# The recurrent mixer's 1/(1 - t): an exponential and a Newton step instead of RECIPROCAL

## The chip, the core and the metric

The kernel runs on one core of one Trainium2 chip. The metric is the device time of one execution in microseconds (us), as the median of several runs. The core has a matrix engine (TensorE, called PE in the profile, with its weight loads as PEld), a vector engine (VectorE, DVE), an engine for activation functions (ScalarE, ACT), a general engine (GpSimd, POOL) and a queue that issues transfers (SyncE, SP). Each engine works off its own instructions in the order in which they were queued; semaphores hold an instruction until what it needs is done, and everything behind it on that engine waits with it.

## What the reference computes

One layer on x of 1024 tokens by 1024 channels, in float32: an RMS norm, one projection `h @ w_in`, two mixers, a gated merge, an output projection and the residual. The first mixer is attention with compressed, selected and windowed keys (8 heads, 2 groups). The second is the recurrent mixer, on which the change works:

```python
uc = conv_b + sum(up[:, k:k + S] * conv_w[k] for k in range(CONV_WIDTH))
r = jax.nn.sigmoid(einsum(ub, lru_wa) + lru_ba)
i = jax.nn.sigmoid(einsum(ub, lru_wx) + lru_bx)
log_a = (-LRU_C * r) * jax.nn.softplus(-lru_lambda)
a = jnp.exp(log_a)
b = jnp.sqrt(-jnp.expm1(2.0 * log_a)) * (i * uc)
h_t = a_t * h_(t-1) + b_t
```

Its output is gated by silu and projected. 512 channels are four blocks of 128.

## The kernel before, in words

Every product is made of three matmuls on parts of float32 numbers, high and low (`mm3`, L169 to L172): high by high, high by low, low by high. `wload` (L174) fetches raw weights over the SP queue, `wsplit` (L179) splits them in two parts on ACT (L184) and on POOL or DVE (L185).

The program has these stages. First x is loaded, normed and transposed (to about 30 us of the span). Then come the recurrent mixer and the compressed keys, interleaved by hand in the order `ORD = "0c1c0c2c1c323"` (L45, L447): each digit takes the generator `lru(n)` of one block of 128 channels to its next `yield`, and `c` does so for `compress()`. The first half of `lru(n)` projects u and the gate, convolves, and splits uc in uh and ul (L336, L337). The second half makes the two gates r and i by matmuls into two PSUM banks named ps_t and a sigmoid each (L352), and then the element-wise chain that the change edits (L353 to L369), on tiles of 128 x 1024. With t = tanh(log_a / 2) (L356), a is (1 + t) / (1 - t) (L363) and sqrt(1 - a^2) is 2 sqrt(-t) / (1 - t) (L357, L364); 1 / (1 - t) is a subtraction (L361) and a RECIPROCAL (L362), both on DVE. Then i is multiplied by uc on POOL (L365) and by the square root on DVE (L366), the scan runs on DVE (L367), POOL multiplies by the gate (L368), and a transfer stores the block (L369). Tiles `t` (the helper `ta`) share nine buffers; the tile `kTs`, which holds the gate and i of a block, has one buffer, so block n + 1 waits for L368 of block n.

Then `qkv(0)` (L469) makes queries, keys and values of the first group, a token block at a time, from block 7 down to block 0, into five PSUM banks used in turn (four ps_s, one ps_f), two a token block. A bank is free when ACT (L498, L499) and DVE (the small copy of the branch gates, L500) have read it. `prep` (L522) takes each token block on: squares on ACT (L531), a sum on DVE (L533), an inverse root on POOL (L192, L193), scalings on DVE and POOL (L536 to L538), splits (L541 to L550), and transposes on PE (L554, L561) with copies on ACT and DVE (L556, L565). When the blocks 3 to 7 are prepared, the first attention scores follow (L612); the attention, with other products between as filling, lasts to about 700 us, and the merge and the output projection end the program. The bias tiles that the scores need are loaded over SP (L454, L458) into buffers of the name t.

What decides the order on every engine is not the program text alone: the context is opened with `schedule_with_timeline_sim=True` (L1103), a planner that orders the instructions by priority (place in the program) and by a timeline of its own. A changed instruction or dependence can so move others. Table loads on ACT (the functions that it can compute at a time) are put in where the order needs them.

Of the kernel before, what the change touches and what calls it, by code (L numbers as in the profile page):

```python
# [9 lines left out]
FT = mybir.dt.float32  # L10
FR = mybir.dt.float32r
AF = mybir.ActivationFunctionType
OP = mybir.AluOpType
# [29 lines left out]
LE = 1  # L43
IE = 0
# [5 lines left out]
CE = 0  # L50
# where the p of the units after the fourth lie in one tile
OFF = {(2, 1): 2560, (1, 1): 1536, (1, 0): 2560, (0, 1): 3584}
# [34 lines left out]
def _build(ctx, tc, A, out, dbg):  # L87
    nc = tc.nc
    dbg = dbg or {}
    V, C, G, T = nc.vector, nc.scalar, nc.gpsimd, nc.tensor  # L90
# [16 lines left out]

# [1 line left out]
    @contextmanager  # L109
# [17 lines left out]
    def ps_f(most):  # L127
        """the banks of the products beside the attention; more of them after it"""
        if tail:
            return next(tail[0])()[:, 0:most]  # L130
        return (ps("ps_f", PF) if PF else ps_s())[:, 0:min(most, FW)]
# [4 lines left out]
    def rotation():  # L136
        """the banks of scores and of those products, in turn"""
        n = PB[0] + PF
        return itertools.cycle([(lambda: ps("ps_f", PF)) if k * PF // n != (k + 1) * PF // n else ps_s for k in range(n)])
# [5 lines left out]

    # after the attention: banks and blocks that it held
    tail = []
# [31 lines left out]
    def wsplit(raw, k, into=None, E=None):  # L179
        """hi and lo parts of 1024 weights per partition, as [128, k, n]"""  # L180
        if into is None:
            into = [ST.tile([128, WTOK], FR, name=n, bufs=2)[:, :raw.shape[-1]] for n in ("w_hi", "w_lo")]
        hi, lo = into
        C.activation(hi, raw, AF.Copy)  # L184
        (E or (V if tail else G)).tensor_tensor(out=lo, in0=raw, in1=f(hi), op=OP.subtract)  # L185
        return [x.rearrange("p (k n) -> p k n", k=k) for x in (hi, lo)]
# [7 lines left out]

# [1 line left out]
    ident_r = K.tile([128, 128], FR, name="ident_r")  # L196
# [43 lines left out]

# [1 line left out]
    kcT = K.tile([128, 2, 2, 64], FR, name="kcT")  # L242
    vcc = K.tile([128, 2, 2, 64], FR, name="vcc")
    # the norms of heads are taken of sums, not means: (sum + 64 eps) ** -0.5. The queries' scale takes
    # the missing factor 8, the keys' gain gets it
    V.tensor_scalar(out=part["kgain"], in0=part["kgain"], scalar1=HD ** 0.5, scalar2=None, op0=OP.mult)
# [6 lines left out]
    def chunk_half(o, wh, wl, half):  # L253
        """o [128, 512] = w^T h^T, tokens of one half"""
        t = slice(half * 512, (half + 1) * 512)
        for kc in range(8):
            mm3(o, wh[:, kc], wl[:, kc], hT_h[:, kc, t], hT_l[half][:, kc], kc == 0, kc == 7)
# [9 lines left out]

# [1 line left out]
    rows_t = DR.tile([NH, NROW], FT, name="rows")  # L269
# [3 lines left out]
    for c0 in range(0, NROW, 512):  # L273
# [8 lines left out]
        dma(rows_t[:, c0:c0 + w], neg)  # L282
# [1 line left out]
    lp = part["lru_p"].rearrange("p (a n) -> p a n", n=4)  # L284
# [13 lines left out]

    # -4 softplus(-lambda): log1p by the series of atanh
    y = K.tile([128, 8, 4], FT, name="spt")  # L300
# [14 lines left out]
    m4sp = K.tile([128, 4], FT, name="m4sp")  # L315
    V.tensor_scalar(out=m4sp, in0=y[:, 5], scalar1=-8.0, scalar2=None, op0=OP.mult)

# [1 line left out]
    yb = DR.tile([4, 128, S], FT, name="yb")  # L319

    def lru(n):
# [31 lines left out]
        sc = m4sp[:, n:n + 1]  # L353
        # t = tanh(log_a / 2): a = (1 + t) / (1 - t), sqrt(1 - a^2) = 2 sqrt(-t) / (1 - t)
        a, q = ta(), ta()
        C.activation(a, r, AF.Tanh, scale=sc)  # L356
        C.activation(q, a, AF.Sqrt, scale=-1.0)  # L357
        if LE == 2:
            C.activation(r, a, AF.Copy, scale=-1.0, bias=1.0)
        else:  # L360
            EN[LE].tensor_scalar(out=r, in0=a, scalar1=-1.0, scalar2=1.0, op0=OP.mult, op1=OP.add)  # L361
        V.reciprocal(r, r)  # L362
        V.scalar_tensor_tensor(out=a, in0=a, scalar=1.0, in1=r, op0=OP.add, op1=OP.mult)  # L363
        V.scalar_tensor_tensor(out=q, in0=q, scalar=2.0, in1=r, op0=OP.mult, op1=OP.mult)  # L364
        EN[IE].tensor_tensor(out=i, in0=i, in1=uc, op=OP.mult)  # L365
        EN[JE >> n & 1].tensor_tensor(out=i, in0=i, in1=q, op=OP.mult)  # L366
# [4 lines left out]

# [1 line left out]
    def compress():  # L373
# [7 lines left out]
        for j in range(2):  # L381
# [3 lines left out]
            for g in range(2):  # L385
# [3 lines left out]
                for b in range(2):  # L389
                    # token 16 (c + b) + 2 l  # L390
                    dv = d.rearrange("p (c l s) -> p c l s", l=8, s=2)
                    V.tensor_tensor(out=flat[b][:, :, g, 0:63].rearrange("p l c -> p c l"),
                                    in0=dv[:, b:b + 63, :, 0],
                                    in1=pe[:, j, None, b * 8:(b + 1) * 8].to_broadcast([128, 63, 8]), op=OP.add)
# [54 lines left out]

# [1 line left out]
    bias = K.tile([128, NH, 256], FT, name="bias")  # L451
# [17 lines left out]
    def qkv(g):  # L469
        """q and the keys and values of both branches, tokens on partitions"""  # L470
        big = fr(p_slc())
# [12 lines left out]
        for tb in range(NT - 1, -1, -1):  # L484
# [21 lines left out]
            yield 0.655  # L506
        # sigmoid(z) = (1 + tanh(z / 2)) / 2: tanh is in every table that the neighbours use
        C.activation(bg[:, g], bg[:, g], AF.Tanh, scale=0.5)
# [13 lines left out]
    def prep(g, tb, e=None):  # L522
        """norms, the split in two parts and the transposes of one token block"""
        if e is None:
# [53 lines left out]
    def scores(g, i, br, st):  # L578
        """p [128, 4 heads, n keys] and the jobs that fill it, one per head; those of the first
        branch fill the compressed branch's p too"""  # L580
        b0 = max(0, i - 4) if br else 0
# [21 lines left out]
        def job(h):  # L603
# [4 lines left out]
            for c0, c1 in zip(cuts, cuts[1:]):  # L608
                s = ps_s()[:, 0:c1 - c0]
                for hl in range(2):  # L610
                    rhs = kT[1][hl][:, b0 * 128 + c0:b0 * 128 + c1] if br else kTs[:, hl, c0:c1]
                    T.matmul(s, qT[h][:, i * 128:(i + 1) * 128], rhs, start=(hl == 0), stop=(hl == 1))  # L612
                # the columns of s by where their bias comes from
                cc = 0
# [46 lines left out]
    def tr(p, c0):  # L661
        """p^T of 128 keys of the four heads, in two parts"""
        pt = ps_t()
# [9 lines left out]
    def tr_c(pc):  # L673
        """p^T of the compressed keys of the four heads: high parts over low parts"""
        pt = ps_t()
# [30 lines left out]
    def units(g):  # L706
        """(jobs, steps) of each unit; a step is a transpose and the product that follows it"""
        for i in range(NT - 1, -1, -1):
# [34 lines left out]
    def gated(half, y1):  # L743
        """y_a^T, gated, in two parts, tokens of one half"""
        tk = slice(half * 512, (half + 1) * 512)
# [14 lines left out]
    def merge(half, pa, m1, ya):  # L760
        """(y_a, projected, + the other mixer's part)^T, tokens of one half"""
        tk = slice(half * 512, (half + 1) * 512)
# [29 lines left out]
    def side_work():  # L792
        """products that wait for nothing: gates, then the recurrent mixer's projection"""
        seq = [("b", m) for m in range(8)] + [("n", m) for m in range(4)] + [("a", m) for m in range(8)]
# [5 lines left out]
        def more():  # L800
            """the next weights in two parts, and the load of those two after them"""
            c = len(ws)
# [6 lines left out]
        more()  # L809
        # by pairs at the end, the first half of the tokens first: what follows needs its place  # L810
        order = [(c, h) for c in range(18) for h in range(2)] + [(c, h) for h in range(2) for c in (18, 19)]
        for c, half in order:
# [4 lines left out]
            while q < 512:  # L817
# [4 lines left out]
                for kc in range(8):  # L822
                    mm3(o, wh[:, kc], wl[:, kc], hT_h[:, kc, t], hT_l[half][:, kc, tl], kc == 0, kc == 7)
                    if kc < 7:
                        yield w * 0.00126
                # tanh(z / 2) of a gate, z of g_nsa
                with urgent(UPE):
# [29 lines left out]
        for t4 in range(4):  # L857
# [23 lines left out]
            more()  # L881
        # the merge of the second half, whose attention ends first
        d2 = [t_l(0, 4), t_l(1, 4)]
# [34 lines left out]
    def attention():  # L918
# [12 lines left out]
        n = len(seq) // 2  # L931
        # the scores that go with the steps of each: those of the next
        ahead = {k: [k + 1] for k in range(2 * n)}
# [98 lines left out]

# [1 line left out]
def _bucket_table():  # L1034
    """which bucket each column of the bias rows takes, and where it is masked"""
    d = np.concatenate([np.arange(NF) - 127,
# [70 lines left out]
```

## Time and profile before

| what | value |
|---|---|
| timed runs | 908.88, 909.04 and 909.33 us, median 909.04 |
| profiled execution | span 908.0 us from the first to the last instruction; no time of its own beside the span is recorded, the median is 1.04 us above it |
| PE busy | 874.2 us, 96% of the span |
| DVE, ACT, POOL busy | 573.3, 439.1, 300.6 us |
| granted TensorE clock, mean | 0.994 of full speed |

Busy PE is not PE at its peak, since matmuls overlap. What is read from the profile is where PE stands idle, which wait ended last there, and what the engine that ended it was doing.

### The profile page before, as it was taken

How to read it: one execution, taken by the hardware profiler on the slowest of the kernel's cores; microseconds unless marked ns; L12 is line 12 of the kernel's file. 1: busy time of each engine (PE TensorE's matmuls, PEld its weight loads, DVE VectorE, ACT ScalarE, POOL GpSimd, SP SyncE). 2: the span in 40 equal slices, each digit the busy share in tenths (PEclk: the TensorE clock that was granted, in tenths of full speed). 3: DMA queues.
4: the chain of work that ended last, by engine and by line, in shares of the span. 5: the costliest groups of instructions: out<-in, count | busy, mean ns of one | idle time of the engine just before them, and what ended most of it. 6: DMA issues, size and time to landing. Idle time of an engine off the chain costs nothing.

```text
span 908.0 us, 15833 instructions
## 1 busy us (share of the span) xinstructions
PE 874.2 (96%) x5670; PEld 781.0 (86%) x5670; DVE 573.3 (63%) x1626; ACT 439.1 (48%) x1159; POOL 300.6 (33%) x339
## 2 busy tenths in 40 slices
PE   4999999989899999999999999999999899999998
PEld 3678878889899999999999998999999877888887
DVE  5642778897722447475687867677777886784111
ACT  6421434645523548575566666566667663321000
POOL 4122233169622325252455553243233421000000
PEclk9999999999999999999999999999999999999999
DMA  9215321121312112122121232111113469983111
GB/s 340 64 49 139 131 95 55 55 82 48 117 48 82 59 48 74 52 86 69 55 66 65 77 102 75 47 54 60 46 42 119 132 202 331 336 270 119 70 70 47
DMA packets 45519, 92.49 MB, mean 102 GB/s; under 512 B 6896, under 2 KB 12704, under 8 KB 45440
## 3 DMA queue, kind: packets, MB, share of 16 engines
q1 hardware_dynamic: 44480, 88.33, 28.9%
q0 software_dynamic: 960, 3.15, 0.9%
q8 instruction: 44, 0.72, 0.3%
q14 instruction: 35, 0.29, 0.1%
HBM read 64.15 MB, written 25.21 MB: 98 GB/s over the span
## 4 chain that ended last, share of the span: by engine, by line
PE 80%; DVE 7%; DMA 4%; POOL 4%; issue 2%; ACT 2%; SPq 0%; DVEq 0%; ACTq 0%; POOLq 0%
PE ps_f L170 9%; PE ps_f L171 9%; PE ps_f L172 9%; PE ps_s L612 7%; PE ps_s L170 7%; PE ps_s L171 7%; PE ps_s L172 7%; PE ps_t L665 6%; PE ps_t L170 4%; PE ps_t L171 4%; PE ps_t L172 4%; PE ps_o L690 3%; PE ps_o L689 3%; POOL ss L193 1%; DVE sq L536 1%
## 5 line engine op out<-in xcount | busy, mean ns | idle before, releaser
L171 PE MATMUL ps_f<-big_l,w_hi 128*128 128x256 f32 (+1 forms) x700 | 200.3, 286 | 0.0
L170 PE MATMUL ps_f<-big_h,w_hi 128*128 128x256 f32 (+1 forms) x664 | 193.8, 292 | 1.0 <-ACT ev L829 0.8
L172 PE MATMUL ps_f<-big_h,w_lo 128*128 128x256 f32 (+1 forms) x664 | 189.4, 285 | 0.0
L171 PEld LDWEIGHTS ps_f<-big_l,w_hi 128*128 128x128 f32 x700 | 131.9, 188 | 2.1
L170 PEld LDWEIGHTS ps_f<-big_h,w_hi 128*128 128x128 f32 x664 | 125.6, 189 | 4.1 <-ACT ev L829 2.3
L172 PEld LDWEIGHTS ps_f<-big_h,w_lo 128*128 128x128 f32 x664 | 125.4, 189 | 1.6
L670 DVE TENSOR_TENSOR pl<-ps_t,ph 128x512 fp32r<-128x512 f32 x132 | 90.4, 686 | 47.5 <-ACT ph L669 46.0
L185 POOL TENSOR_TENSOR w_lo<-w_raw,w_hi 128x1024 fp32r<-128x1024 f32 x33 | 80.7, 2448 | 102.1 <-ACT w_hi L184 101.7
L669 ACT ACTIVATE ph<-ps_t 128x512 fp32r<-128x512 f32 x132 | 78.1, 599 | 48.8 <-PE ps_t L665 45.6
L650 POOL TENSOR_SCALAR p_slc<-p_slc,mx,bg 128x384 f32<-128x384 f32 (+7 forms) x88 | 68.7, 786 | 89.5 <-DVE mx L649 34.8
L646 ACT ACTIVATE p_slc<-ps_s,mx 128x256 f32<-128x256 f32 (+5 forms) x128 | 68.1, 541 | 24.1 <-DVE mx L644 18.6
L171 PE MATMUL ps_s<-big_l,w_hi 128*128 128x512 f32 (+1 forms) x184 | 73.8, 401 | 0.0
L184 ACT ACTIVATE w_hi<-w_raw 128x1024 fp32r<-128x1024 f32 (+1 forms) x40 | 42.4, 1062 | 43.6 <-PE ps_f L171 17.5
L636 DVE TENSOR_REDUCE mx<-ps_s 128x1 f32<-128x256 f32 (+5 forms) x120 | 50.9, 436 | 11.0 <-PE ps_s L612 9.3
L170 PE MATMUL ps_s<-big_h,w_hi 128*128 128x512 f32 x136 | 55.3, 408 | 2.5 <-ACT big_h L237 2.5
L689 PE MATMUL ps_o<-ph,t 128*128 128x512 f32 x132 | 55.7, 422 | 0.0
L650 POOL TENSOR_SCALAR p_win<-p_win,mx,bg 128x640 f32<-128x640 f32 (+1 forms) x40 | 34.7, 869 | 59.3 <-DVE mx L649 25.5
L665 PE MATMUL ps_t<-ident_r,p_slc 128*128 128x128 f32 x336 | 54.2, 273 | 0.0
L612 PE MATMUL ps_s<-kTs,t 128*128 128x512 f32 (+4 forms) x224 | 53.0, 349 | 0.6 <-ACT pc L621 0.3
L172 PE MATMUL ps_s<-big_h,w_lo 128*128 128x512 f32 x136 | 53.5, 397 | 0.0
L641 DVE CUSTOM_DVE_ANT_0 ps_s<-ps_s,bias 128x256 f32<-128x256 f32 (+1 forms) x128 | 52.5, 417 | 1.4 <-PE ps_s L612 0.3
L690 PE MATMUL ps_o<-pl,t 128*128 128x512 f32 x132 | 53.2, 403 | 0.0
(331 smaller groups left out, 2213.3 us busy)
## 6 DMA issues: line engine op xcount, KB each, us to landing
w_raw<-in_w_in SPq DMA_DIRECT2D x30, 512.0 KB
t<-in_x SPq DMA_DIRECT2D x8, 512.0 KB
gb<-ev SPq DMA_DIRECT2D x16, 256.0 KB
ga<-ev SPq DMA_DIRECT2D x16, 256.0 KB
w_raw<-in_w_out SPq DMA_DIRECT2D x8, 512.0 KB
st<-mb SPq DMA_DIRECT2D x16, 256.0 KB
w_raw<-in_w_tok SPq DMA_DIRECT2D x6, 524.0 KB
ev<-in_cw SPq DMA_DIRECT2D x8, 256.0 KB
```

What stands on the lines that cost most here:

```text
L170: T.matmul(o, lh, rh, start=first, stop=False)
L171: T.matmul(o, lh, rl, start=False, stop=False)
L172: T.matmul(o, ll, rh, start=False, stop=last)
L185: (E or (V if tail else G)).tensor_tensor(out=lo, in0=raw, in1=f(hi), op=OP.subtract)
L612: T.matmul(s, qT[h][:, i * 128:(i + 1) * 128], rhs, start=(hl == 0), stop=(hl == 1))
L646: C.activation(p[:, h, k0:k1], sv, AF.Exp, bias=mx[:, 6:7], accum_out=mx[:, 7 + j:8 + j])
L650: G.tensor_scalar(out=p[:, h], in0=p[:, h], scalar1=mx[:, 9:10], scalar2=bg[:, g, i, 4 * (br + 1) + h:4 * (br + 1) + h + 1], op0=OP.mult, ...
L665: ins = T.transpose(pt[:, h * 128:(h + 1) * 128], p[h][:, c0:c0 + 128], ident)
L669: C.activation(ph, pt, AF.Copy)
L670: V.tensor_tensor(out=pl, in0=pt, in1=f(ph), op=OP.subtract)
L689: T.matmul(o, vf, pp[0], start=first, stop=False)
L690: T.matmul(o, vf, pp[1], start=False, stop=False)
```

## The change

`lru(n)` no longer takes the reciprocal. 1 / (1 - t) equals (1 + exp(log_a)) / 2, so ACT computes exp(m8sp * r) in place of r and then 0.5 x + 0.5 as a copy; one Newton step, two scalar_tensor_tensor instructions on DVE, follows: uc = (t - 1) * r, r = (uc + 2) * r. The tile uc holds the intermediate, so the POOL product of i and uc is written ahead of it. The square root moves behind the two new ACT instructions. A small constant m8sp is made once.

```diff
     m4sp = K.tile([128, 4], FT, name="m4sp")
     V.tensor_scalar(out=m4sp, in0=y[:, 5], scalar1=-8.0, scalar2=None, op0=OP.mult)
+    m8sp = K.tile([128, 4], FT, name="m8sp")
+    V.tensor_scalar(out=m8sp, in0=y[:, 5], scalar1=-16.0, scalar2=None, op0=OP.mult)
...
         a, q = ta(), ta()
         C.activation(a, r, AF.Tanh, scale=sc)
+        EN[IE].tensor_tensor(out=i, in0=i, in1=uc, op=OP.mult)
+
+        C.activation(r, r, AF.Exp, scale=m8sp[:, n:n + 1])
+        C.activation(r, r, AF.Copy, scale=0.5, bias=0.5)
         C.activation(q, a, AF.Sqrt, scale=-1.0)
-        if LE == 2:
-            C.activation(r, a, AF.Copy, scale=-1.0, bias=1.0)
-        else:
-            EN[LE].tensor_scalar(out=r, in0=a, scalar1=-1.0, scalar2=1.0, op0=OP.mult, op1=OP.add)
-        V.reciprocal(r, r)
+        V.scalar_tensor_tensor(out=uc, in0=a, scalar=1.0, in1=r, op0=OP.subtract, op1=OP.mult)
+        V.scalar_tensor_tensor(out=r, in0=uc, scalar=2.0, in1=r, op0=OP.add, op1=OP.mult)
         V.scalar_tensor_tensor(out=a, in0=a, scalar=1.0, in1=r, op0=OP.add, op1=OP.mult)
         V.scalar_tensor_tensor(out=q, in0=q, scalar=2.0, in1=r, op0=OP.mult, op1=OP.mult)
-        EN[IE].tensor_tensor(out=i, in0=i, in1=uc, op=OP.mult)
         EN[JE >> n & 1].tensor_tensor(out=i, in0=i, in1=q, op=OP.mult)
```

`LE` is 1 here, so the subtraction was on DVE; `IE` is 0, so the product of i and uc is on POOL. The rest of the diff takes out comments.

## Rows read from the trace of the kernel before

**Rows 1.** Busy time of each engine in stretches of the span (start and end, length, then busy us and number of instructions for each engine, the granted clock, the share of DMA, GB/s).
```profile
110.00:190.00 80.00, 79.45 (x450) 67.21 (x448) 67.34 (x50) 36.69 (x54) 22.90 (x13) 1.00 0.24 77
190.00:250.00 60.00, 53.10 (x412) 51.80 (x412) 48.12 (x90) 31.80 (x97) 46.38 (x52) 0.94 0.21 71
250.00:700.00 450.00, 448.39 (x3404) 424.09 (x3403) 287.17 (x1145) 265.33 (x806) 175.88 (x200) 1.00 0.20 67
700.00:908.00 208.00, 197.74 (x971) 163.44 (x969) 111.47 (x266) 59.05 (x137) 24.58 (x39) 1.00 0.50 172
...
240.00:250.00 10.00, 9.89 (x70) 9.69 (x71) 5.34 (x22) 5.78 (x18) 1.82 (x4) 0.83 0.30 105
```

**Rows 2.** Waits of PE (who waited, for whom, us in total, times, longest): the first four between 180 and 300 us, the last from the stretch before 120 us.
```profile
PE ps_s L170 <- DVE bg L500: 2.8, 1, 2.8
PE ps_s L612 <- ACT t L565: 2.4, 1, 2.4
PE ps_f L170 <- DVE bg L500: 0.7, 1, 0.7
PE ps_t L561 <- DVE t L556: 0.6, 1, 0.6
...
PE ps_t L419 <- DVE t L414: 0.5, 1, 0.5
```

**Rows 3.** PE's instructions in order of time (start, us, line, tile, idle time before it and who ended it). The matmuls between 197.41 and 200.46 start every 0.218 us (14 steps), those from 200.82 to 203.15 every 0.123 us (19 steps).
```profile
176.46 0.50 PE L170 MATMUL ps_t<-t,bias 128*128 128x512 f32 x1
...
196.15 0.39 PE L170 MATMUL ps_s<-w_hi,big_h 128*128 128x262 f32 x1 [2.80 <-DVE bg L500]
...
197.41 0.42 PE L170 MATMUL ps_s<-w_hi,big_h 128*128 128x262 f32 x1
...
200.46 0.40 PE L172 MATMUL ps_s<-p_slc,big_l 128*128 128x262 f32 x1
...
200.82 0.28 PE L171 MATMUL ps_f<-w_lo,big_h 128*128 128x262 f32 x1
...
203.15 0.29 PE L172 MATMUL ps_f<-p_slc,big_l 128*128 128x262 f32 x1
```

**Rows 4.** DVE's instructions in order of time.
```profile
181.12 0.16 DVE L500 COPY bg<-ps_s 128x12 f32<-128x12 f32 x1
...
183.39 6.54 DVE L362 RECIPROCAL t<-t 128x1024 f32<-128x1024 f32 x1
189.86 2.22 DVE L367 TENSOR_TENSOR_SCAN t<-t,kTs 128x1024 f32<-128x1024 f32 x1
...
192.58 2.71 DVE L536 TENSOR_TENSOR sq<-ev,ss 128x384 f32<-128x384 f32 x1
...
195.94 0.16 DVE L500 COPY bg<-ps_s 128x12 f32<-128x12 f32 x1
...
236.58 2.76 DVE L536 TENSOR_TENSOR sq<-ev,ss 128x384 f32<-128x384 f32 x1 [1.50 <-POOL ss L193]
```

**Rows 5.** ACT's instructions in order of time: the table loads around the square root of the third block, and what follows.
```profile
172.05 1.28 ACT L357 ACT_TABLE_LOAD   x1
173.34 1.06 ACT L357 ACTIVATE t<-t 128x1024 f32<-128x1024 f32 x1
174.42 1.28 ACT L352 ACT_TABLE_LOAD   x1
175.71 0.69 ACT L352 ACTIVATE kTs<-ps_t,small 128x512 f32<-128x512 f32 x1
...
195.88 1.27 ACT L352 ACTIVATE kTs<-ps_t,small 128x512 f32<-128x512 f32 x2
...
239.58 0.27 ACT L565 CAST t<-ps_t 128x128 fp32r<-128x128 f32 x1 [4.44 <-DVE kTs L565]
```

**Rows 6.** POOL's instructions in order of time.
```profile
176.54 2.44 POOL L365 TENSOR_TENSOR kTs<-kTs,t 128x1024 f32<-128x1024 f32 x1 [19.34 <-ACT kTs L352]
...
183.62 1.35 POOL L193 TENSOR_TENSOR ss<-ss,nhalf 128x6 f32<-128x6 f32 x1
192.21 2.66 POOL L368 TENSOR_TENSOR t<-t,kTs 128x1024 f32<-128x1024 f32 x1 [7.24 <-issue]
...
200.94 2.41 POOL L365 TENSOR_TENSOR kTs<-kTs,t 128x1024 f32<-128x1024 f32 x1
...
236.51 2.41 POOL L185 TENSOR_TENSOR p_slc<-w_raw,p_slc 128x1048 fp32r<-128x1048 f32 x1
```

**Rows 7.** The instructions of one line each: number, duration in ns (min, median, max), first and last start.
```profile
L361 DVE TENSOR_SCALAR t<-t x4: 679/694/694, 101.8 to 181.2; 128x1024 f32<-128x1024 f32 x4
...
L362 DVE RECIPROCAL t<-t x4: 6540/6552/6553, 102.5 to 183.4; 128x1024 f32<-128x1024 f32 x4
...
L363 DVE SCALAR_TENSOR_TENSOR t<-t x4: 1209/1982/3473, 114.6 to 197.0; 128x1024 f32<-128x1024 f32 x4
...
L356 ACT ACTIVATE t<-t,m4sp x4: 1137/1151/1152, 100.6 to 178.3; 128x1024 f32<-128x1024 f32 x4
...
L336 ACT ACTIVATE t<-t x4: 1059/1060/1061, 62.3 to 165.3; 128x1024 fp32r<-128x1024 f32 x4
```

**Rows 8.** ACT's table loads by the line of the instruction that needs them (number, then us in total, mean ns of one, idle time before): the one of the attention's exponentials.
```profile
L646 ACT ACT_TABLE_LOAD x1 | 1.3, 1283 | 0.0
```

**Rows 9.** A wait of the SP queue between 90 and 260 us (who waited, for whom, us in total, times, longest).
```profile
SPq L454 <- DVE t L364: 12.0, 1, 12.0
```

## The prediction, made before the result was known

> **What bounds the kernel now.** I read the page's busy times first, then the busy times by stretch, PE's waits, and then each engine's instructions around the places where PE waits. The busy times (in the table above) have PE far ahead of the others; by stretch it is busy 778.7 of the 798 us from 110 us on [rows 1], so a change on DVE and ACT can only win back time in which PE stands. The stretches show where that is: in the 80 us from 110, where three of the four reciprocals lie, PE idles 0.55 us; in the 60 us from 190 it idles 6.9 us; in the 450 us of attention 1.6 us; at the end 10.3 us, 500 us after the edit [rows 1]. So the reciprocals matter only through what the last ones leave behind for the stretch 190 to 250.
>
> PE's waits name the places there [rows 2]: 2.8 us for the gate copy L500 on DVE, 0.7 us for another L500, 0.6 us for L556, 2.4 us for the first scores (L612). The first is the edit's: PE has no free bank for the matmul that goes on at 196.15, after 2.80 us [rows 3]. DVE made a gate copy at 181.12 and the next at 195.94; between them lie the last block's RECIPROCAL (183.39, 6.54 us), the third block's scan and a scaling of prep [rows 4]. That gap of 14.8 us cost 2.8 us, so five banks carry PE through a gap of about 12 us. After the stall the matmuls start every 0.218 us instead of every 0.123 us until 200.46 [rows 3]: 14 steps of 0.095 us, 1.3 us more.
>
> The second place is the first scores. They wait for L565 on ACT at 239.58, which had waited 4.44 us for DVE [rows 5]; DVE was held by POOL's L193 and then by a 2.76 us L536 [rows 4] that ran beside POOL's L185 [rows 6]. POOL is the engine of this stretch beside PE, 46.4 of 60 us busy [rows 1]. And POOL stood 7.24 us before L368 at 192.21 [rows 6], which multiplies the result of the scan that started at 189.86, right behind the RECIPROCAL of another block [rows 4]. So one reciprocal holds both the banks and POOL's queue.
>
> **The change part by part.** Removed from DVE, for each of four blocks: 0.69 + 6.55 = 7.24 us [rows 7], 29.0 us in all. Added to DVE: two scalar_tensor_tensor. The same form and size at L363 took 1.21 us at least, 1.98 in the middle, 3.47 at most [rows 7]; so 2.4 to 6.9 us a block. I take 1.21 each, since two stand back to back with nothing else of the block due, and keep 3.47. DVE is lighter by 7.24 - 2.42 = 4.8 us a block (0.3 at the worst). m8sp is one instruction on 128 x 4 elements, once, in the start-up; a copy of 128 x 12 takes 0.16 us [rows 4], so its cost is under 0.2 us even if nothing covers it, and I take 0.
>
> Added to ACT: the exponential, like the tanh of the same size 1.15 us, and the copy, like L336 1.06 us [rows 7]. The square root brings a table load of 1.28 us in front and the next sigmoid another [rows 5]; the first exponential of the attention (L646), which follows this stage's sigmoids, brought one too [rows 8], so the new one brings at least one more, and a sigmoid that falls between exponential and square root a fourth. So 3.5 to 4.8 us a block. ACT is busy 36.7 of 80 us there [rows 1], which hides it by sum.
>
> The moved square root starts 2.2 us and a load later. L364, which needs it, now stands behind the Newton step and L363, 3 x 1.21 = 3.6 us after the copy; load and square root take 2.3 us, so it is hidden by 1.3 us. No moved step issues a transfer. On SP the bias loads stand 12.0 us for L364 of the third block [rows 9]; L364 ends near 183.8 in the sum below, some 2.5 us later, and nothing that PE needs before 240 us is behind them: nothing.
>
> The moved POOL product makes a new wait: the Newton step overwrites uc, so DVE can't begin before L365 is done. Behind it on DVE stand gate copies and prep. For the third block L365 ends at 176.54 + 2.44 = 178.98 [rows 6]. From there DVE needs five instructions of 1.21 us (Newton, L363, L364, L366) and the scan of 2.22 [rows 4]: 187.3, with a gate copy and a sum between about 188.0. POOL's L368 then starts 4.2 us before its 192.21. With the Newton at 3.47 each it would be at 192.5: nothing.
>
> One more place on PE: the gate matmul of the last block at 176.46 takes the ps_t bank that the sigmoid at 175.71 frees at 176.40 [rows 3, 5]; there is no slack. Two table loads and a square root already stood ahead of that sigmoid without costing PE anything, so I take 0; two more loads would be 2.6 us, which I keep as the upper bound.
> The Trainium skill (ScalarE: Activation LUTs, Table sets: the hidden batching unit) says that exp and sqrt lie in different sets and that a switch costs about 2.7 us, which speaks against a square root behind an exponential; the trace shows 1.28 us and the next function 0.01 us behind it [rows 5]. By the page's figure that upper bound would be an estimated 5.3 us and the gain below could be lost.
>
> Sum on the path: the stall, 2.8; the slow matmuls behind it, 1.3; a wait of 0.5 at L414 near 114 us, behind DVE's first reciprocal [rows 2]. PE reaches the first scores 4.6 us earlier; the chain through POOL that feeds them is 4.2 us earlier, so 0.4 is given back there. Gain 4.2 us (bounds: 0 with the dear Newton, minus 2.6 if ps_t stalls too; 9.4 with all waits of 190 to 250 gone). Span 908.0 - 4.2 = 903.8; the median lies 1.04 us above the span, so **904.8 us**. After 250 us PE has next to no idle time to swallow this [rows 1]; the planner re-orders, which I count at 1 to 2 us either way.
>
> **The rivals.** First, more goes than the one stall: POOL's 7.24 us come back in full and the first scores find their keys ready. Then 2.4 + 0.7 + 0.6 us of waits go [rows 2], and the slow clock (0.83 on the mean in 240 to 250 [rows 1]: 3.4 us at half clock, of which 1 - 0.123/0.218 is lost, 1.5 us): 5.2 us more, 899.6. For it: that idle stretch is longer than the 4.2 us counted. Against: the scores hang on DVE's queue order, which is planned anew.
>
> Second, it is given back: PE arrives 4.6 us earlier at the first scores and waits there, as POOL is no earlier. A two-input instruction on DVE and POOL in the same stretch lengthen each other: L536 took 2.76 us beside L185. RECIPROCAL did not do this: POOL's L193 took 1.35 us beside it [rows 6]. Eight new two-input instructions bring that. It decides where the Newton step takes nearly 3.47 us an instruction; the time is then 908.5, no change.
> The Trainium skill (SBUF — State Buffer, Who interferes with whom) has this as a rule: a DVE instruction with two SBUF inputs and a GpSimd instruction that reads SBUF exclude each other, one with a single input outside its two-port modes does not; the rows agree.
>
> Third, slower: DVE stands at the last block's Newton step. That block's L365 needs i, whose sigmoid waits for the third block's L368: before, sigmoids at 195.88, L365 at 200.94 to 203.35, 8.5 us after L368's end at 194.87 [rows 5, 6]. With L368 ending at 188.0 + 2.7 = 190.7, L365 ends between 195.4 (no queue on POOL: the sigmoids' end at 197.15 is 2.3 us behind L368's, and L365 takes 2.4) and 199.2. If the planner puts the Newton step directly behind the third block's scan, as it put the RECIPROCAL directly ahead of it, the next gate copy comes at 197.8 to 201.6, a gap of 16.5 to 20.3 us since 181.3. Beyond 14.8 us it is worse than before: PE stalls 4.5 to 8.3 us in place of 2.8, prep is late with it, and the time is 909.0 + 3.6 = 912.6. Against: a planner that sees the dependence queues other work first.
>
> **How the numbers follow.** Forecast 0.52, all waits gone 0.12, given back 0.18, slower 0.18. A change under 0.2% (1.8 us) can't be told from none here. Faster takes the first two, less 0.01 for the forecast's own edge (902 to 907.5): 0.63. Same 0.18, slower 0.19. The range leaves out the last rival, which begins at 910.9, and reaches to the first one's 899.6: 899 to 911.
>
> **What would show it.** Right: no RECIPROCAL of 128 x 1024; DVE's total down by 13 to 19 us; ACT's up by 14 to 19 with at least four more table loads; between 181 and 196 no two gate copies more than 12 us apart, no PE wait for L500 there, clock 1.00 in 190 to 200; L368 of the third block near 188. The forecast is wrong if PE waits longer than 2.4 us at the first L612, at ps_t L170 near 176 us or for L500 behind a Newton step, or if the waits after 250 us (1.6 and 10.3 us now) grow by more than 2 us.

## The result: slower, and the profile after

The changed kernel takes 917.03 us (median of 4 runs, 916.92 to 917.57); the kernel before, run beside it, 909.06 us (908.88 to 909.33). The ratio is 1.0086 (95% interval 1.0071 to 1.0100). Forecast were 904.8 us and a range of 899 to 911: wrong in sign. The profiled execution has a span of 915.2 us, 7.2 more than before.

Line numbers move by two or so: the gates' sigmoids are L354, the Tanh L358, POOL's product i*uc L359 (L365 before), the exponential L361, the Copy L362, the square root L363, the Newton step L364 and L365, the scan L369, POOL's last product L370 (L368 before), the compression's product L416 with the matmul L421 behind it, the gate copy L502.

First the page's busy times of the changed kernel, and its busy times by stretch, with the columns of [rows 1].

```profile
PE 875.6 (96%) x5670; PEld 782.0 (85%) x5670; DVE 552.1 (60%) x1627; ACT 456.3 (50%) x1174; POOL 301.4 (33%) x339
...
110.00:190.00 80.00, 73.01 (x364) 60.39 (x364) 44.82 (x40) 42.00 (x59) 21.65 (x11) 0.92 0.18 58
190.00:250.00 60.00, 52.81 (x415) 51.86 (x413) 47.48 (x73) 32.73 (x85) 46.77 (x48) 0.94 0.24 76
...
140.00:150.00 10.00, 10.00 (x66) 8.72 (x65) 0.35 (x1) 9.91 (x12) 1.71 (x1) 1.00 0.17 59
150.00:160.00 10.00, 6.75 (x22) 5.11 (x22) 9.24 (x8) 1.62 (x4) 3.07 (x2) 0.66 0.00 0
...
180.00:190.00 10.00, 7.72 (x47) 7.07 (x46) 0.50 (x2) 9.86 (x13) 2.37 (x1) 0.86 0.00 0
```

The edit does what it says: DVE has 21.2 us less to do, ACT 17.2 more. The loss lies where the kernel before had next to none. From 110 to 190 us PE idles 7.0 us instead of 0.55 [rows 1], at a mean clock of 0.92 instead of 1.00; from 190 to 250 it idles 7.2, about as before. Of the 7.2 us of span 5.8 are idle time of PE (39.6 against 33.8 us in all) and 1.4 are PE being busy longer. The ten-us rows point at ACT: from 140 to 150 and from 180 to 190 ACT is busy 9.9 of 10 us and DVE 0.35 and 0.50. Where the forecast saw a DVE that holds the others up, it now has nothing to do because ACT gives it nothing.

PE's waits of the changed kernel between 100 and 250 us (columns as in [rows 2]):

```profile
PE ps_t L563 <- DVE t L558: 4.8, 1, 4.8
PE ps_t L421 <- DVE t L416: 3.2, 1, 3.2
PE ps_t L170 <- ACT kTs L354: 2.3, 1, 2.3
PE ps_t L556 <- ACT kTs L354: 2.1, 1, 2.1
PE ps_t L439 <- ACT t L433: 1.5, 1, 1.5
```

The two waits that the forecast set out from, 2.8 us for the gate copy and 2.4 us at the first scores [rows 2], are gone. Five others are there; L421, L170 and L439 make up the 7.0 us of the stretch from 110 us, the other two 7.0 of the 7.2 us behind 190. ACT's instructions around the third block's Tanh, in order of time, show why; [rows 5] is the same place before:

```profile
176.18 1.15 ACT L358 ACTIVATE t<-t,m4sp 128x1024 f32<-128x1024 f32 x1
177.35 1.28 ACT L361 ACT_TABLE_LOAD   x1
178.64 1.15 ACT L361 ACTIVATE t<-t,m8sp 128x1024 f32<-128x1024 f32 x1
179.81 1.28 ACT L354 ACT_TABLE_LOAD   x1
181.11 0.69 ACT L354 ACTIVATE kTs<-ps_t,small 128x512 f32<-128x512 f32 x1
181.82 1.28 ACT L363 ACT_TABLE_LOAD   x1
183.11 1.06 ACT L363 ACTIVATE t<-t 128x1024 f32<-128x1024 f32 x1
184.08 1.04 ACT L362 ACTIVATE t<-t 128x1024 f32<-128x1024 f32 x1
185.14 1.28 ACT L354 ACT_TABLE_LOAD   x1
186.43 0.69 ACT L354 ACTIVATE kTs<-ps_t,small 128x512 f32<-128x512 f32 x1
```

Four table loads, where [rows 5] has two: the gate i comes in two halves (the tile kTs), and each half's sigmoid stands behind a function of another set. i's second half starts 10.25 us behind the Tanh's start; before it was 6.9 us here (168.80 to 175.71). That is 3.3 us in this block, and the block itself starts 7.4 us later than before. PE's 2.3 us at ps_t L170 end at 187.17, when that sigmoid frees its bank. POOL's and DVE's instructions show what i's second half holds up:

```profile
148.29 2.41 POOL L359 TENSOR_TENSOR kTs<-kTs,t 128x1024 f32<-128x1024 f32 x1 [9.72 <-ACT kTs L354]
150.68 2.40 POOL L185 TENSOR_TENSOR p_slc<-p_win,p_slc 128x1048 fp32r<-128x1048 f32 x1
...
187.26 2.37 POOL L359 TENSOR_TENSOR kTs<-kTs,t 128x1024 f32<-128x1024 f32 x1 [21.70 <-ACT kTs L354]
...
204.74 2.39 POOL L370 TENSOR_TENSOR t<-t,kTs 128x1024 f32<-128x1024 f32 x1
...
227.31 2.34 POOL L370 TENSOR_TENSOR t<-t,kTs 128x1024 f32<-128x1024 f32 x1
```

```profile
121.69 2.39 DVE L431 TENSOR_TENSOR t<-t,small 64x128 f32<-64x128 f32 x1
...
148.44 0.35 DVE L416 SCALAR_TENSOR_TENSOR t<-ps_s,small,t 128x128 f32<-128x128 f32 x1 [12.10 <-ACT t L415]
150.73 3.42 DVE L364 SCALAR_TENSOR_TENSOR t<-t 128x1024 f32<-128x1024 f32 x1 [1.94 <-POOL kTs L359]
154.08 0.34 DVE L416 SCALAR_TENSOR_TENSOR t<-ps_f,small,t 128x128 f32<-128x128 f32 x1
...
188.28 0.17 DVE L502 COPY bg<-ps_s 128x12 f32<-128x12 f32 x1 [11.99 <-ACT ev L501]
189.67 1.22 DVE L364 SCALAR_TENSOR_TENSOR t<-t 128x1024 f32<-128x1024 f32 x1 [1.22 <-POOL kTs L359]
...
199.84 2.28 DVE L369 TENSOR_TENSOR_SCAN t<-t,kTs 128x1024 f32<-128x1024 f32 x1
...
227.37 2.69 DVE L538 TENSOR_TENSOR sq<-ev,ss 128x384 f32<-128x384 f32 x1 [1.50 <-POOL ss L193]
229.98 0.28 DVE L558 CAST t<-ps_t 128x128 fp32r<-128x128 f32 x1
```

In all four blocks the Newton step L364 waits for POOL's product, since it overwrites uc (1.2 to 1.9 us, 6.8 in all). In the second block it then takes 3.42 us, beside POOL's L185 that had started 0.05 us earlier; the second compression product stands behind it until 154.08, and PE, at L421, stands 3.25 us until 154.47; its granted clock is 0.66 on the mean from 150 to 160. DVE stood 12 us until 188.28, because the copies of ACT for which L502 waits (L500 and L501, at 187.59 and 187.86) were queued behind the same sigmoids; PE's last matmul before them started at 184.61. PE's wait of 1.5 us at L439 lies ahead of these: L431, a DVE instruction of the compression, takes 2.39 us beside POOL's first L370 (121.56, 2.37 us), where the same instruction takes 0.27 us in e2 below. POOL's L370 comes at 121.56, 163.14, 204.74 and 227.31 us in the four blocks, before at 120.71, 154.81, 192.21 and 211.60: 0.9, 8.3, 12.5 and 15.7 us late. The lateness is handed on, because the next block's L345 writes the single buffer of kTs that L370 reads, as ACT's row of the last block shows:

```profile
207.16 1.08 ACT L345 ACTIVATE kTs<-ps_s 128x512 f32<-128x512 f32 x2 [1.90 <-POOL t L370]
208.13 1.27 ACT L354 ACTIVATE kTs<-ps_t,small 128x512 f32<-128x512 f32 x2
```

The sigmoids behind it free the bank for which PE waits 2.1 us, until 208.88. At the end the last L370 falls on the prep of the attention: L538 beside it takes 2.69 us (0.64 us in the middle of its eight), as L536 did beside POOL in [rows 4], and PE's 4.8 us end with L558 behind it. Some 2.1 of them are this lengthening and 1.50 DVE's wait for POOL's L193; how much of the rest is the lateness isn't separated.

### The profile page after: what moved, and what is told of

It is laid out like the page before. It is cut to its first block, busy times and chain, and to the rows that moved or that the text cites. A ratio compares the mean times of both kernels' runs of the same rounds, so it can differ in the third digit from the quotient of the medians.

```text
span 915.2 us, 15847 instructions
## 1 busy us (share of the span) xinstructions
PE 875.6 (96%) x5670; PEld 782.0 (85%) x5670; DVE 552.1 (60%) x1627; ACT 456.3 (50%) x1174; POOL 301.4 (33%) x339
## 4 chain that ended last, share of the span: by engine, by line
PE 70%; ACT 5%; POOL 4%; DVE 3%; issue 3%; DMA 1%; SPq 0%; ACTq 0%; POOLq 0%; DVEq 0%
PE ps_f L170 9%; PE ps_f L171 8%; PE ps_f L172 8%; PE ps_s L614 7%; PE ps_t L667 6%; PE ps_s L170 5%; PE ps_s L171 5%; PE ps_s L172 5%; PE ps_t L170 3%; PE ps_t L171 3%; PE ps_t L172 3%; PE ps_o L691 3%; PE ps_o L692 3%; POOL ss L193 1%; POOL kTs L359 1%
## 5 line engine op out<-in xcount | busy, mean ns | idle before, releaser
L170 PE MATMUL ps_f<-big_h,w_hi 128*128 128x256 f32 (+1 forms) x664 | 193.1, 291 | 1.0 <-ACT ev L831 0.8
L170 PEld LDWEIGHTS ps_f<-big_h,w_hi 128*128 128x128 f32 x664 | 124.7, 188 | 4.1 <-ACT ev L831 2.2
L185 POOL TENSOR_TENSOR w_lo<-w_raw,w_hi 128x1024 fp32r<-128x1024 f32 x33 | 80.4, 2440 | 101.9 <-ACT w_hi L184 101.6
L170 PE MATMUL ps_s<-big_h,w_hi 128*128 128x512 f32 x136 | 56.7, 418 | 0.4 <-ACT big_h L237 0.4
```

What stands on the lines that cost most here:

```text
L170: T.matmul(o, lh, rh, start=first, stop=False)
```

## The experiments

Three theories. **T**: the table loads of the exponential (and it and the Copy themselves) stand on ACT ahead of i's second sigmoid, and this is late. **W**: the Newton step overwrites uc, so DVE and the scan hang on POOL's product. **P**: neither; the edit only led to another order of the queues, and any edit of this kind could cost as much. Times are medians; each ratio is against runs of the kernel before on the same chip, whose medians were 909.1 to 909.6 us, so differences between runs of separate chips carry up to 0.6 us. e1, e4 and e5 leave out the start value of the Newton step: e1 and e5 put a Tanh in its place, e4 takes r itself.

| run | us | ratio, 95% interval | POOL's last product, third block |
|---|---|---|---|
| before | 909.1 | | 192.2 |
| changed | 917.0 | 1.0071 to 1.0100 | 204.7 |
| e1, Tanh for the exponential | 909.8 | 0.9992 to 1.0011 | 195.8 |
| e2, Newton in a tile of its own | 908.3 | 0.9975 to 0.9994 | 189.4 |
| e3, ACT's part alone | 923.0 | 1.0132 to 1.0162 | 212.1 |
| e4, DVE's part alone | 906.1 | 0.9954 to 0.9979 | 188.8 |
| e5, e1 and e2 | 901.1 | 0.9904 to 0.9932 | 183.4 |
| e6, exponential behind the gates | 907.8 | 0.9979 to 0.9999 | 191.8 |
| e7, e6 and e2 | 909.0 | 0.9989 to 1.0006 | 189.9 |
| e8, gates as Tanh | 910.0 | 0.9997 to 1.0017 | 190.3 |
| e9, e8 and e2 | 905.4 | 0.9940 to 0.9964 | 186.2 |
| e10, e9 with root times uc | 910.8 | 0.9995 to 1.0023 | 191.2 |
| e11, e9 with 1 + Tanh on ACT | 908.3 | 0.9975 to 0.9993 | 186.7 |
| e12, e11, compression as Tanh | 915.5 | 1.0056 to 1.0081 | 192.7 |

The last column goes with the time only loosely: e12 has nearly the 192.2 of before and takes 915.5 us.

**No table change for the exponential (e1).**

```diff
-        C.activation(r, r, AF.Exp, scale=m8sp[:, n:n + 1])
+        C.activation(r, r, AF.Tanh, scale=m8sp[:, n:n + 1])
```

> The changed kernel with Tanh in place of Exp in the new ScalarE instruction: same size, same queue, but a function of the table that the gates' sigmoids already use, so no table load for it (1/(1 - t) starts from a wrong value; this part of the result is left out). Theory T (the table loads: two more a block stand ahead of the second sigmoid of i, and all that hangs on it is late): two loads a block as before the change, i's second sigmoid about 7.5 to 8 us behind the start of L358 in place of 10.25, the waits of PE at ps_t L170 (2.3) and L421 (3.2) shrink below 1 us, time 906 to 911. Theory W (the Newton step overwrites uc and so stands on VectorE for POOL's product): the wait stays, time 914 to 917. Theory P (the planner's new order costs by itself): no change from 917.

Measured 909.78 us: the same number of ACT instructions of the same sizes, but two loads a block, and 7.2 us come back. ACT in the first block, in order of time:

```profile
99.43 1.15 ACT L358 ACTIVATE t<-t,m4sp 128x1024 f32<-128x1024 f32 x1
100.61 1.15 ACT L361 ACTIVATE t<-t,m8sp 128x1024 f32<-128x1024 f32 x1
101.86 0.69 ACT L354 ACTIVATE kTs<-ps_t,small 128x512 f32<-128x512 f32 x1
...
103.51 1.28 ACT L363 ACT_TABLE_LOAD   x1
...
105.89 1.28 ACT L354 ACT_TABLE_LOAD   x1
107.18 0.69 ACT L354 ACTIVATE kTs<-ps_t,small 128x512 f32<-128x512 f32 x1
```

i's second half comes 7.75 us behind the Tanh, 2.5 earlier than in the changed kernel: two loads. Leave the table loads out, and PE, DVE, ACT and POOL run the same instructions in the same order in both profiles, from the first to the last. So the seven loads alone are worth 7.2 of the 8 us, and theory P has no part in them. PE keeps 2.1 us at L421 and 3.8 at L563, the waits that W explains, but also 2.1 (L556) and 1.4 (L170) for i's sigmoids; T had expected L170 and L421 below 1 us.

**A tile of its own for the Newton step (e2).** The first result goes into two free half tiles. With the tie the order of other instructions on the engines changes too, so what this run shows is the two together.

```diff
-        V.scalar_tensor_tensor(out=uc, in0=a, scalar=1.0, in1=r, op0=OP.subtract, op1=OP.mult)
-        V.scalar_tensor_tensor(out=r, in0=uc, scalar=2.0, in1=r, op0=OP.add, op1=OP.mult)
+        for h_, nm in enumerate(("eo", "ep")):
+            nt = te2(nm)
+            c_ = slice(h_ * 512, (h_ + 1) * 512)
+            V.scalar_tensor_tensor(out=nt, in0=a[:, c_], scalar=1.0, in1=r[:, c_], op0=OP.subtract, op1=OP.mult)
+            V.scalar_tensor_tensor(out=r[:, c_], in0=nt, scalar=2.0, in1=r[:, c_], op0=OP.add, op1=OP.mult)
```

> The changed kernel, but the Newton step's intermediate goes into two half tiles of its own (buffers that the attention uses later), so it no longer waits for POOL's product of i and uc; four instructions of 512 columns in place of two of 1024. Theory W: VectorE no longer idles 1.2 to 1.9 us before L364, L416 comes early, PE's 3.2 us at L421 goes, time 906 to 911. Theory T: the table loads stay (eight in the gates and around the square root more than before the change), ps_t L170 still costs PE about 2 us, time 913 to 917. Theory P: 917, or anything, with other waits.

Measured 908.31 us with all the loads of the changed kernel: 8.7 us come back. That is W's forecast for this run, as e1 gave T's for the other; each alone missed in the other's run. PE's largest wait between 100 and 250 us is now T's:

```profile
PE ps_t L170 <- ACT kTs L354: 3.3, 2, 2.3
PE ps_t L559 <- DVE st L547: 2.0, 2, 1.1
PE ps_t L424 <- DVE t L419: 1.8, 1, 1.8
```

**ACT's part alone (e3)**: the kernel before with its RECIPROCAL, and exponential and Copy written into r ahead of it.

```diff
...
         C.activation(a, r, AF.Tanh, scale=sc)
+        C.activation(r, r, AF.Exp, scale=m8sp[:, n:n + 1])
+        C.activation(r, r, AF.Copy, scale=0.5, bias=0.5)
         C.activation(q, a, AF.Sqrt, scale=-1.0)
...
```

> The kernel before the change with only the ScalarE part added: exponential and copy over r between Tanh and Sqrt; the subtraction and RECIPROCAL overwrite their result, so the output is that of before. VectorE's work is that of before. Theory T: ScalarE's order is that of the changed kernel, i's second sigmoid 10 us behind the tanh, PE waits at ps_t L170 near 180 us; time 913 to 919. Theory W: POOL's product is awaited by L366 alone, as before the change; time 909 to 911. Theory P: between, no wait at ps_t.

923.03 us: 13.4 us slower, without any Newton step, and 4 us beyond T's range. What the forecast held to be hidden is the dearest part of the edit. Added to e4 below, the same two instructions a block cost 10.9 us (906.1 to 917.0). PE's waits: 4.2 us behind the compression, 3.8 for a copy on ACT, 2.9 for i's sigmoid.

```profile
PE ps_t L423 <- DVE t L418: 4.2, 1, 4.2
...
PE ps_s L170 <- ACT ev L502: 3.8, 1, 3.8
PE ps_t L170 <- ACT kTs L354: 2.9, 2, 2.3
```

**DVE's part alone (e4)**: the changed kernel without exponential and Copy.

> The changed kernel without exponential and copy (the Newton step starts from r itself; its result is wrong, and this part is left out): only the VectorE part of the change, with POOL's product ahead of it. Theory T: two table loads a block, second sigmoid of i 6 to 7 us behind the tanh; the gain that was forecast appears, 903 to 908. Theory W: VectorE still stands for POOL's product, PE still waits at L421 and L563; 912 to 917. Theory P: 909 to 917 with waits at new places.

906.09 us, 3.5 us better than the runs beside it (forecast for the whole edit: 4.2). POOL's instructions in the third block:

```profile
176.45 2.41 POOL L359 TENSOR_TENSOR kTs<-kTs,t 128x1024 f32<-128x1024 f32 x1 [16.73 <-ACT kTs L354]
...
188.79 2.37 POOL L368 TENSOR_TENSOR t<-t,kTs 128x1024 f32<-128x1024 f32 x1
```

The product begins at 176.45 (176.54 before [rows 6]) and the last product at 188.79, where the forecast had 188.0. So its DVE half stands. The Newton step waits for POOL up to 9.6 us here, 22.2 us in all, and the kernel is still faster: the length of DVE's standing doesn't set the loss. That the standing costs e4 nothing is not shown: e5 below, with a tile of its own, is 5.0 us faster though it has two ACT instructions a block more, and e4 was not run with such a tile.

**Both causes away (e5)**: the edits of e1 and e2.

> Both of the first two edits at once: Tanh in place of Exp (no table load for it; 1/(1 - t) starts from a wrong value, that part of the result is left out) and a tile of its own for the Newton step's intermediate. If the two causes lie in series (the table loads make i's second sigmoid and so POOL's product late; the Newton step waits for that product), either edit alone frees nearly all, and this is 905 to 908, little below the 908.3 of the own tile. If they cost independently of each other, each its 8 us, it is 899 to 902.

901.14 us, 15.9 under the changed kernel; e1 took away 7.2 and e2 8.7, the sum is 15.9. So the two costs add up. Again the order on all four engines is the same in e2 and e5 but for the loads, and these are again worth 7.2 us (908.3 to 901.1). PE's waits between 100 and 250 us:

```profile
PE ps_s L170 <- DVE kTs L346: 2.4, 1, 2.4
PE ps_t L566 <- DVE t L570: 0.8, 1, 0.8
PE ps_t L559 <- DVE st L547: 0.7, 1, 0.7
```

**The exponential behind the gates (e6), and with a tile of its own (e7).** In the first three blocks exponential, Copy and square root are issued behind i's second sigmoid.

```diff
+                sig_i = C.activation(g_[:, t], s, AF.Sigmoid, bias=b_[:, n:n + 1])
...
+        with tc.issue_after(sig_i.ins) if n < 3 else ExitStack():
+            C.activation(r, r, AF.Exp, scale=m8sp[:, n:n + 1])
+            C.activation(r, r, AF.Copy, scale=0.5, bias=0.5)
+            C.activation(q, a, AF.Sqrt, scale=-1.0)
```

> The changed kernel, whole, with one more order on ScalarE: in the first three blocks exponential, copy and square root are queued behind the second sigmoid of i, so ScalarE changes its table three times a block in place of four and i is early (2.5 us behind the start of L358). uc is still shared. Theory T (late i through table loads): L354's second sigmoid early, no wait at ps_t L170 near 180 us, POOL's product 7 us earlier than in the changed kernel, 904 to 908. Theory W (the wait on POOL's product itself, whenever it comes): 912 or more. Theory P (planner's new order): around 915 with other waits.

> The pinned order and the tile of its own together; computes everything. With i early the Newton step has nothing to wait for in the first three blocks; what is left is the last block, whose i waits for the gate tile. Series: within 2 us of the pinned kernel alone, 903 to 907. Independent: 900 or less.

907.84 and 909.03 us: three loads a block, and i's product early (172.23 in the third block of e6). That takes 9.2 us off the changed kernel without touching the Newton step, as T says; but W's wait goes with it, since the Newton step's own inputs now come behind i: in e6 DVE waits for the product once only, 1.4 us. So the tile of its own adds nothing in e7, which misses both of its ranges, and the two costs don't add up in this order: W costs where the exponential stands ahead of i. Other waits of PE have come in e6, 2.7 us for a gate copy and 2.1 for a sigmoid of r; what they are worth was not separated.

**The gates as Tanh (e8, e9).** sigmoid(z) = (1 + tanh(z/2)) / 2, the factors in the small constants; the product (1 + tanh) * uc moves from POOL to DVE. The whole of the computation is kept. e9 has the tiles of e2 as well.

```diff
-                C.activation(g_[:, t], s, AF.Sigmoid, bias=b_[:, n:n + 1])
+                C.activation(g_[:, t], s, AF.Tanh, scale=0.5, bias=b_[:, n:n + 1])
...
-        EN[IE].tensor_tensor(out=i, in0=i, in1=uc, op=OP.mult)
...
+        V.scalar_tensor_tensor(out=i, in0=i, scalar=1.0, in1=uc, op0=OP.add, op1=OP.mult)
...
-        C.activation(r, r, AF.Exp, scale=m8sp[:, n:n + 1])
...
+        C.activation(r, r, AF.Exp, scale=sc, bias=sc)
```

> The changed kernel with the three sigmoids of the recurrent mixer written as tanh (sigmoid(z) = (1 + tanh(z/2)) / 2, the halves folded into scales, biases and the constants of the instructions behind), so that gates, tanh and exponential can use one table and only the square root changes it; the product of i and uc becomes (tanh + 1) * uc in one instruction on VectorE, so POOL has none. Theory T: fewer loads than eight around L361 to L363 less, i's second sigmoid 7 to 8 us behind L358, 904 to 909. If the loads are not what costs, it stays at 912 or more, as VectorE has 1.2 us a block more than in the changed kernel.

> The changed kernel with both causes taken away and the whole of the computation kept: both gates as (1 + tanh(z/2)) / 2 (factors put into the small constants), so that gates, Tanh and Exp need no change of table among them, and the Newton step's first result in two half tiles of its own, so that it overwrites nothing that the product i*uc reads. The product (tanh + 1) * uc is on VectorE, 1.2 us a block more there. Theory T+W (late second gate half by table loads, and the wait for the product, each for itself): two loads a block, second half of i at most 8 us behind the Tanh, no wait of Newton on a product; time 901 (the Tanh kernel with tiles of its own) to 904, the product on VectorE being what it costs over that kernel. W alone (the wait is the whole cost): as the kernel with tiles of its own, 908. Order alone (P): 907 to 911, like the other kernels with another order.

910.01 and 905.37 us, 1.0 and 1.4 us above T's ranges. e9 is faster than both kernels (ratio to before 0.9952, 0.9940 to 0.9964), 11.7 us under the changed one. Not all loads that were to go are gone: i's second half is 7.75 us behind the Tanh in the first block, as in e1, but 9.0 in the second and third. There the compression's sigmoid had changed the table before; the gates and the Tanh ran without a load, and the exponential brought one, here in the third:

```profile
169.17 1.28 ACT L362 ACT_TABLE_LOAD   x1
```

e9 stays 4 us above e5, with these waits of PE, the first for a gate copy on the DVE that now also carries the product:

```profile
PE ps_s L170 <- DVE bg L506: 3.7, 1, 3.7
PE ps_t L170 <- ACT kTs L355: 1.6, 1, 1.6
```

**Three tries to win those 4 us.** e10: POOL multiplies uc into the square root, DVE joins i by (tanh + 1) * q, and the compression's sigmoid is written as Tanh too. e11: e9, but a Copy on ACT forms 1 + tanh, and the product is POOL's again. e12: e11 and the compression as in e10.

```diff
+        C.activation(i, i, AF.Copy, bias=1.0)
+        EN[IE].tensor_tensor(out=i, in0=i, in1=uc, op=OP.mult)
...
-                C.activation(sg[:, hf], z, AF.Sigmoid, bias=cb1[:, j, hf:hf + 1])
+                C.activation(sg[:, hf], z, AF.Tanh, scale=0.5, bias=cb1h[:, j, hf:hf + 1])
+                V.tensor_scalar(out=sg[:, hf], in0=sg[:, hf], scalar1=0.5, scalar2=0.5, op0=OP.mult, op1=OP.add)
```

> As the kernel before it, but GpSimd multiplies uc into the square root, which needs no gate, instead of VectorE into i; i joins by (tanh + 1) * q on VectorE, in place of the product i*q. The compression's sigmoid is also (1 + tanh) / 2, which saves its loads. VectorE has then as much to do as in the changed kernel, and neither engine waits for i's second half until the last product before the scan. T+W: 899 to 903, at or below the one before it; loads in these stretches: two a block, for the root and back. If the product's wait is the root's instead (the root is the last of ScalarE's functions, 1.3 us of load ahead of it): no better than the one before it, with VectorE waiting for GpSimd's product ahead of the scan.

> As e9 (both gates as tanh, the Newton step's first result in tiles of its own), but 1 + tanh(z_i/2) is formed by a Copy on ScalarE (1.05 us a block, no load of its own seen so far for Copy) and the product with uc goes back to GpSimd. So VectorE has 1.2 us a block less than in e9, ScalarE 1.05 more, behind i's second half. If what separates e9 (905.4) from the Tanh kernel with own tiles (e5, 901.1) is VectorE's extra product, this comes to 901 to 903. If it is the order that comes out, or the gates' loads in the compression's stretch, it stays at 904 to 908. If ScalarE's queue is what sets the end here also when no load stands in it, 906 or more.

> As e11, and the compression's sigmoid too as (1 + tanh) / 2, which saves its loads (two of 1.28 us, and those back) for one more short operation on VectorE each time. If those loads count, 1 to 2 us below e11; if not, the same as e11 within 1 us; in e10 the same edit stood beside another order and 910.8, so above 906 would say that the compression's part itself costs.

910.84 us (906.2 to 913.3, the widest spread of all), 908.28 and 915.53: none comes below e9. e11 falls in the last case of its expectation, so DVE's extra product is not simply what separates e9 from e5. By e12 against e11 the compression's edit, with the order that it brings, costs 7.3 us although it saves four loads. DVE in e12, in order of time:

```profile
109.67 2.44 DVE L423 TENSOR_SCALAR t<-t 128x128 f32<-128x128 f32 x1
111.96 1.21 DVE L373 SCALAR_TENSOR_TENSOR t<-t 128x1024 f32<-128x1024 f32 x1
...
114.23 0.21 DVE L423 TENSOR_SCALAR t<-t 128x128 f32<-128x128 f32 x1
```

The added short instruction stands in DVE's queue once beside POOL's product and once behind two long ones; PE's matmul of the compression behind it stands 2.1 us until 114.8 and 3.8 until 154.4 (the profile names no releaser). P falls for the loads, whose 7.2 us come twice at an unchanged order. For W it stays open how much of the 8.7 us is the tie itself and how much the order that changes with it. e10 and e11 lie several us above what T and W gave; that this is the order is argued, not shown.

## Why the prediction was wrong, step by step

**DVE lighter: right.** Forecast 19.2 us in four blocks. RECIPROCAL and 1 - t took 29.0 us [rows 7] and are gone. Seven of the eight Newton instructions took 1.21 to 1.23 us, one 3.42: 12.0 us against 9.7 forecast. L363, 8.6 us in the four blocks before, is 4.9 as L366. In all 21.2 us less, a little over the 13 to 19 that were given as the sign. e4 shows what it is worth, with the moved product: 3.5 us.

**ACT's addition "hidden by sum": this step failed.** Its size was right: 17.2 us, 14 to 19 forecast, seven more loads where at least four were. Its place was not. The forecast compared a sum with the mean of a stretch, 36.7 of 80 us [rows 1], and didn't ask what stands behind the new instructions in ACT's queue. The fourth load, a sigmoid between exponential and root, was named as possible; that this sigmoid and the next are the gate i, for which POOL, DVE and PE's bank wait, was not followed. The 2.6 us for PE's bank, kept as a bound and set to 0 in the sum, came out as 2.3 us, one of five waits. It stays below the 2.4 us that were to show the forecast wrong, and the waits at L421, L556 and L563 were not among its signs; of its signs of being right, L368 near 188 and a clock of 1.00 from 190 to 200 failed (L370 at 204.74, clock 0.97).
The Trainium skill (ScalarE: Activation LUTs, Table sets: the hidden batching unit) tells to group functions by set; the trace agrees, as e1, with the same number of instructions in one set fewer, is 7.2 us faster. The 2.66 us that the Trainium skill (ScalarE: Activation LUTs, What ACT_TABLE_LOAD costs) gives for a switch is not seen in these rows: a load takes 1.28 us, begins 0.02 us behind the function before it, and the next function starts 0.02 us behind it.

**POOL's product of the third block at 176.54 as before: failed with it.** It came at 187.26. From the product's end to L370 the forecast counted 188.0 - 178.98 = 9.0 us; e4, where the product is in time, took 9.9 (178.86 to 188.79), the changed kernel 15.1 (189.63 to 204.74), since prep that had queued up stands between the block's instructions on DVE and POOL. Taken as a fixed start, the product also hid that a block hands its delay to the next by the single kTs buffer.

**The stall of 2.8 us goes: right, but not a gain.** The gate copy's wait and that at the first scores are gone (two gate copies, at 188.28 and 197.98, are 9.7 us apart, where 12 were the most allowed); 4.8 us at L563 and 2.1 at L556 stand in their stretch.

**The root hidden by 1.3 us: right.** It ends at 184.17, and L367, which needs it, starts at 193.67.

**The rivals.** The slower one had the right instruction, a Newton step that stands on POOL's product, but named the last block alone and 912.6 us. It stands in all four, for 6.8 us, and in e4 for 22.2 us in a faster kernel; so the length of the standing isn't the price. W is that the Newton step, which needs nothing of i, is tied to a product that the loads make late (8.7 us, e2, with the order that follows). "Given back" had its mechanism in three rows (L431's 2.39 us and L538's 2.69 beside L370, L364's 3.42 beside L185), each with a PE wait behind it.
The Trainium skill (SBUF — State Buffer, Who interferes with whom) has a DVE instruction with two SBUF inputs and a GpSimd instruction that reads SBUF exclude each other; the 3.42 us of L364, which began 0.05 us behind POOL's L185 and took 1.22 us alone, agree.

## What to carry to other kernels

Work moved to an engine isn't free just because that engine's busy share is low: write out that engine's queue with the new instructions and every table load in it, and look for what another engine waits for behind them. Keep functions of one table set together, or choose forms that share a set (Tanh for a sigmoid), counting the loads that other stages' functions bring in between; and give a new intermediate a place of its own, since reusing a dead-looking tile ties the step to its last reader. A chain that runs through blocks by a single buffer hands a delay on: 0.9 us in the first block was 15.7 in the fourth here.

## What the runs showed of the hardware

An instruction of DVE with one tensor input was held up beside POOL as well: in e12 a TENSOR_SCALAR of 128x128 took 2.44 us from 109.67, while POOL's product ran from 109.00 to 111.96, and 0.21 us at 114.23. Copy brought no load of its own in any of these orders. Around PE's 3.25 us of standing, which ended at 154.47, the granted clock is 1.00 from 150 to 153 and 0.50 from 155 to 158, the levels of 2.4 and 1.2 GHz. In the changed kernel PE is busy 1.4 us longer than before for the same 5670 matmuls.
